# A two-layer decoder step on one core: the sample group's retention step split into dot products with the old states and a later rewriting of the states

## The chip, the core and the metric

The kernel runs on one core of one Trainium2 chip. The metric is the device time of one execution in microseconds. Three runs of the kernel before took 2169.92, 2166.01 and 2169.59 us; the median is 2169.59 us.

## What is computed

Two layers of a decoder trunk, width 2048, in float32. A prompt of 512 tokens and a sample group of 8 sequences with one new token each share all weights and go through the matmuls together, 520 columns. In short:

```python
h = rmsnorm(x); z = h @ W_in                      # b, c, xc, g_conv | q, k, v, g_ret
conv branch: y_c = b * conv3(c * xc) * silu(g_conv)
retention, 4 heads of 256: q, k through rope, k also by 1/16
  prompt: chunked retention from a zero state
  sample: S_new = gamma_h * S + k v^T             # S: 256 x 256 for each layer, head, sequence
          o     = q S_new
o = groupnorm(o) * gn_g * silu(g_ret)
x = x + concat(y_c, y_r) @ W_out
x = x + sigmoid(x @ W_pg) * (p @ W_ple)
```

The outputs are the trunk's result after a final RMSNorm, the last rows of the convolution's input, and the new retention states of both groups. The sample group has 2 x 4 x 8 = 64 states of 256 KB, each read and each written. gamma_h is 1 - 2^(-5-h).

## The kernel before

**Matmuls.** Every float32 product is made of three matmuls: weights and operands are split into a rounded high part and the rest, and high*high, high*low and low*high are added in PSUM (`mm3`, lines 247 to 249). A weight chunk of 128x512 comes in by an SP-queue DMA into the `raw` ring, ScalarE makes its high part (`split_w`, line 229), VectorE its low part (line 230); both go into the `split` ring of 60 tiles of 128x128. Pairs of output tiles are computed by `plain` or by `strassen`, which saves one product of eight and needs sums of weights (VectorE, line 319) and of operands (lines 413 to 416). Operands are split by ScalarE (line 551) and VectorE (line 552).

**Stages of a layer.** The four heads (q, k, v, gate tiles, with the prompt's retention steps in between), eight convolution steps, the out phase (`O` times `wo`, eight pairs of output tiles) and the gate phase (`Gt` times `wg`, eight pairs, seven in the second layer). After the second gate phase a tail computes the last two tiles, the final norm and the outputs. In the profile the heads of layer 0 end near 405 us, its convolutions near 725; its out phase near 914 us and its gate phase near 1076; in layer 1 these are near 1440, 1790, 1975 and 2110 us.

**The sample step.** `sample()` is called at set places of the heads and the convolutions. It runs `sample_step` for one state that an earlier call has loaded, and issues the two loads of the next (`sample_load`): the state, and its q and k broadcast to 128 partitions (`kq`). The step multiplies the state by gamma on ScalarE (line 776, 128x512), adds k times v on VectorE (line 780, two halves of 128x256), stores the new state (line 781, `o_rets`) and takes the dot products with q on VectorE (line 784, two halves, sums into `osum`). In the last convolution step the remaining states are worked off and `sample_norm` (lines 1365 to 1390) does the group norm of `osum`: two pairs of matmuls with a matrix of ones, a power on GpSimd (`rsn`, line 1383), and eight small VectorE products into `gs` (line 1389). `retained` copies `gs` into the columns 512 to 519 of the out phase's operands (line 1064), after it has loaded the prompt's part (`ys`, line 1063).

**What sets the order.** A scheduler places the instructions of each engine by a simulated time line; an engine then works through its list in order and waits, at each instruction, for what it needs. Operations marked `keep` stay in program order on their engine. `middle` and `later` hold functions that are called in the course of the next pair: `later` at two places (`aside`), `middle` at one. All loads and stores of activations and states are issued from GpSimd's queue (`SIDE`), which is in order as well. `Slots` is a pool of 75 buffers of 128x520.

## Time and profile before

| | |
|---|---|
| three runs, median (lowest to highest) | 2169.59 us (2166.01 to 2169.92) |
| profiled execution, its own time by the trace: span from the first to the last instruction | 2167.3 us |
| TensorE matmuls (PE) | 2147.8 us busy, 17861 instructions |
| VectorE (DVE) | 1896.1 us busy, 3849 instructions |
| ScalarE (ACT) | 1264.5 us busy, 2647 instructions |
| GpSimd (POOL) | 430.6 us busy, 746 instructions |
| DMA | 387.31 MB, mean 179 GB/s |
| mean granted TensorE clock | 0.999 |

The profiled execution lies within the three runs, 2.3 us below their median. A busy engine is one with an instruction in flight; SP and the issue of a DMA by SP or ACT aren't counted. A group's mean is the length of one instruction from start to end; consecutive ones overlap a little, so that n of them take a little less than n times the mean. In the view of waits a row names the waiting engine and its tile and line, what it waited for, the sum, the number of waits and the longest. In a table of windows the first number is the length of the stretch, then come the busy time of each engine with its instruction count, the clock, the share of DMA time and GB/s.

### The profile page before, as it was taken

The page shows a single profiled execution, that of the slowest core. Times are in us where ns is not written, and L with a number is a line of the kernel's source. Part 1 is how long each engine was busy: PE and PEld are TensorE (multiplying, and loading weights), DVE is VectorE, ACT ScalarE, POOL GpSimd, SP SyncE. Part 2 cuts the span into 40 slices and gives each one's busy share as a digit, 9 for nine tenths or more (in the row PEclk, how much of TensorE's full clock was granted, in tenths as well). Part 3 has the DMA queues.
Part 4 walks back from the last instruction along what each step waited for, and adds up shares of the span by engine and source line. Part 5 has one row for each costly group of instructions (what it writes and reads, how often), then busy time and mean ns, then how long its engine had stood idle before and what let it go on. Part 6 is the DMA issues. An engine that isn't in the chain of part 4 may idle for free. (4 is left out here: it accounts for less than half of the span.)

```text
span 2167.3 us, 48178 instructions
## 1 busy us (share of the span) xinstructions
PE 2147.8 (99%) x17861; PEld 2142.1 (99%) x17861; DVE 1896.1 (87%) x3849; ACT 1264.5 (58%) x2647; POOL 430.6 (20%) x746
## 2 busy tenths in 40 slices
PE   9999999999999999999999999999999999999998
PEld 9999999999999999999999999999999999999998
DVE  8889988998999987987997988989999998879884
ACT  8656655565555655655765655565645555456565
POOL 2313222211001211200212222231111022011011
PEclk9999999999999999999999999999999999999999
DMA  8555565545543745645645566664464355566455
GB/s 288 171 175 197 181 217 184 178 157 175 158 129 118 238 156 187 215 154 160 215 144 175 172 213 191 189 209 170 151 182 149 120 158 202 176 207 200 128 164 198
DMA packets 182861, 387.31 MB, mean 179 GB/s; under 512 B 25888, under 2 KB 56352, under 8 KB 182624
## 3 DMA queue, kind: packets, MB, share of 16 engines
q1 hardware_dynamic: 128704, 212.98, 31.6%
q0 software_dynamic: 53056, 169.84, 23.8%
q8 instruction: 140, 2.29, 0.4%
q10 hardware_dynamic: 864, 1.39, 0.2%
q14 instruction: 97, 0.79, 0.1%
HBM read 318.96 MB, written 65.15 MB: 177 GB/s over the span
## 5 line engine op out<-in xcount | busy, mean ns | idle before, releaser
L247 PE MATMUL ps_g<-slot,split 128*128 128x260 f32 x5465 | 1531.6, 284 | 7.2 <-ACT slot L307 2.9
L248 PE MATMUL ps_g<-slot,split 128*128 128x260 f32 x5465 | 1534.3, 282 | 0.3 <-DVE slot L555 0.3
L249 PE MATMUL ps_g<-slot,split 128*128 128x260 f32 x5461 | 1519.9, 283 | 0.5 <-DVE split L230 0.5
L229 ACT ACTIVATE split<-raw 128x512 fp32r<-128x512 f32 (+2 forms) x1347 | 777.3, 596 | 583.1 <-DVE raw L319 213.2
L247 PEld LDWEIGHTS ps_g<-slot,split 128*128 128x128 f32 x5465 | 1024.0, 188 | 10.1 <-ACT slot L307 3.7
L248 PEld LDWEIGHTS ps_g<-slot,split 128*128 128x128 f32 x5465 | 1028.5, 188 | 0.5 <-DVE slot L555 0.5
L249 PEld LDWEIGHTS ps_g<-slot,split 128*128 128x128 f32 x5461 | 1019.8, 188 | 1.0 <-DVE split L230 1.0
L230 DVE TENSOR_TENSOR split<-raw,split 128x512 fp32r<-128x512 f32 (+2 forms) x1346 | 849.2, 652 | 172.5 <-PE ps_g L248 85.4
L319 DVE TENSOR_TENSOR raw<-raw 128x512 f32<-128x512 f32 (+1 forms) x660 | 428.9, 660 | 32.5 <-DMA raw<-wi 23.7
L307 ACT ACTIVATE slot<-ps_g 128x260 f32<-128x260 f32 x336 | 127.4, 381 | 140.6 <-PE ps_g L249 122.7
L551 ACT ACTIVATE slot<-slot 128x520 fp32r<-128x520 f32 (+1 forms) x212 | 109.2, 562 | 46.6 <-DVE slot L414 11.1
L552 DVE TENSOR_TENSOR slot<-slot,slot 128x520 fp32r<-128x520 f32 (+1 forms) x212 | 124.4, 620 | 4.1 <-ACT slot L551 3.9
L781 POOL DMA_DIRECT2D o_rets<-slot x64 | 35.3, 552 | 351.6 <-DVE slot L780 131.7
L307 DVE TENSOR_TENSOR slot<-ps_g,slot 128x260 f32<-128x260 f32 x168 | 70.9, 424 | 6.0 <-PE ps_g L249 3.7
L869 POOL DMA_DIRECT2D slot<-hs x64 | 46.2, 724 | 118.7 <-DVE split L230 42.7
L814 POOL DMA_DIRECT2D hs<-slot x64 | 35.6, 556 | 139.3 <-DVE slot L755 61.3
L780 DVE SCALAR_TENSOR_TENSOR slot<-slot,vs,slot 128x256 f32<-128x256 f32 x128 | 56.1, 481 | 4.5 <-ACT slot L776 4.3
L746 DVE TENSOR_TENSOR slot<-slot,slot 128x520 f32<-128x520 f32 x80 | 55.8, 698 | 4.7 <-DMA o_rets<-slot 3.7
L770 POOL DMA_DIRECT2D slot<-sret x64 | 35.5, 554 | 114.6 <-ACT split L229 37.3
L1058 POOL DMA_DIRECT2D slot<-x1s x76 | 40.8, 538 | 87.6 <-PE ps_g L249 27.2
L1209 POOL DMA_DIRECT2D x2s<-slot x30 | 16.4, 545 | 201.6 <-DVE slot L1204 200.6
L771 POOL DMA_DIRECT2D slot<-kq x64 | 34.9, 547 | 106.0 <-DVE slot L876 22.2
(217 smaller groups left out, 1733.8 us busy)
## 6 DMA issues: line engine op xcount, KB each, us to landing
raw<-wi SPq DMA_DIRECT2D x377, 256.0 KB, 3.9
raw<-wo SPq DMA_DIRECT2D x128, 256.0 KB, 5.4
raw<-wg SPq DMA_DIRECT2D x122, 256.0 KB, 4.1
raw<-wi SPq DMA_DIRECT2D x136, 192.0 KB, 4.0
slot<-x1s POOLq DMA_DIRECT2D x76, 260.0 KB, 5.1
slot<-sret POOLq DMA_DIRECT2D x64, 256.0 KB, 4.0
hs<-slot POOLq DMA_DIRECT2D x64, 256.0 KB, 4.0
slot<-hs POOLq DMA_DIRECT2D x64, 256.0 KB, 5.2
```

The source lines that it names most:

```text
L229: S.activation(hi, raw, AF.Copy)
L230: V.tensor_tensor(lo, raw, F(hi), SUB)
L247: PE.matmul(out, wh, xh, start=start, stop=False, skip_group_check=more)
L248: PE.matmul(out, wh, xl, start=False, stop=False, skip_group_check=more)
L249: PE.matmul(out, wl, xh, start=False, stop=stop, skip_group_check=more)
L307: fn(*args)
L319: V.tensor_tensor(out[:, n], x[:, n], y[:, n], op)
L551: keep(S.activation(hi, src[:, n], AF.Copy))
L552: V.tensor_tensor(lo, src[:, n], F(hi), SUB)
L746: V.tensor_tensor(out[:, n], v, table[:, n], MUL)
L780: keep(V.scalar_tensor_tensor(st[:, c], k, vs[:, h, e, b : b + 1], st[:, c], MUL, ADD))
L869: SIDE.dma_start(t[:, :512].rearrange("p (m n) -> p m n", m=2), src)
```

## The change

The dot products are taken with the old state, as q (gamma S) + (q . k) v instead of q (gamma S + k v), and the new state is made later, apart from it.

- In the heads and convolutions `sample_load` loads the old state and, for every second state, the q of two sequences; `sample_step` is only the two dot products on VectorE, with gamma as their constant. The ScalarE product, the k v products and the store are gone from here.
- `retain` multiplies q and k element by element (`qk`), and `vs` is divided by gamma. `sample_norm` begins with two matmuls that sum `qk` over the partitions, two products with `vs` (`own`) and two additions to `osum`.
- In the out and gate phases `update()` does one state's new value in three calls one after the other: `key_load` loads the broadcast k into the right half of a slot; `state_add` makes v k / gamma in both halves by two ScalarE copies with a scale, then issues a GpSimd-queue DMA that adds the old state from DRAM into the slot; `state_out` multiplies the slot by gamma on ScalarE and stores it. Each call works on three states, one in each of these steps. It's called at the middle and at the end of each pair, and in the out phase for m = 2, 6, 10, 14 also from `later`.
- The constants gamma are no longer a part of `vec`.

```diff
@@ constants
+GAMMA = [1.0 - 2.0 ** (-5 - h) for h in range(H)]
...
-    def gam(h):
-        return vec[:, 128 + h : 129 + h]
...
+    qk = const.tile([P, 2, H, NS], F32, name="qk")
...
         def sample_load(h, b):
-            st, kb = get(), get()
+            st = get()
             SIDE.dma_start(st[:, :512], sret[l, h, b])
-            SIDE.dma_start(kb[:, :512], kq[l, h, b].rearrange("c d -> (c d)").partition_broadcast(P))
-            return h, b, st, kb
-
-        def sample_step(h, b, st, kb):
-
-            keep(S.activation(st[:, :512], st[:, :512], AF.Identity, scale=gam(h)))
-            k = kb[:, 256:512]
+            if b % 2 == 0:
+                queries.append(get())
+                src = kq[l, h, b : b + 2, :2].rearrange("b c d -> b (c d)").partition_broadcast(P)
+                SIDE.dma_start(queries[-1][:, :512].rearrange("p (b c) -> p b c", b=2), src)
+            return h, b, st, queries[-1]
+
+        def sample_step(h, b, st, q):
+
             for e in range(2):
                 c = slice(256 * e, 256 * e + 256)
-                keep(V.scalar_tensor_tensor(st[:, c], k, vs[:, h, e, b : b + 1], st[:, c], MUL, ADD))
-            SIDE.dma_start(o_rets[l, h, b], st[:, :512])
-            for e in range(2):
-                c = slice(256 * e, 256 * e + 256)
-                V.tensor_tensor_reduce(k, st[:, c], kb[:, :256], 1.0, 0.0, MUL, ADD, osum[:, e, h, b : b + 1])
-            put(st, kb)
-
-        loaded = []
+                n = slice(256 * (b % 2), 256 * (b % 2) + 256)
+                keep(V.tensor_tensor_reduce(st[:, c], st[:, c], q[:, n], GAMMA[h], 0.0, MUL, ADD, osum[:, e, h, b : b + 1]))
+            put(st)
+            if b % 2:
+                put(q)
+
+        loaded, queries = [], []
...
+        def key_load(h, b):
+            st = get()
+            SIDE.dma_start(st[:, 256:512], kq[l, h, b, 2:].rearrange("c d -> (c d)").partition_broadcast(P))
+            return h, b, st
+
+        def state_add(h, b, st):
+            for e in range(2):
+                c = slice(256 * e, 256 * e + 256)
+                keep(S.activation(st[:, c], st[:, 256:512], AF.Copy, scale=vs[:, h, e, b : b + 1]))
+            SIDE.dma_start(st[:, :512], sret[l, h, b], accum_op=ADD)
+            return h, b, st
+
+        def state_out(h, b, st):
+            keep(S.activation(st[:, :512], st[:, :512], AF.Copy, scale=GAMMA[h]))
+            SIDE.dma_start(o_rets[l, h, b], st[:, :512])
+            put(st)
+
+        keyed, added = [], []
+
+        def update():
+
+            if added:
+                state_out(*added.pop(0))
+            if keyed:
+                added.append(state_add(*keyed.pop(0)))
+            if states:
+                keyed.append(key_load(*states.pop(0)))
+
+        states = [(h, b) for h in range(H) for b in range(NS)]
...
+            V.scalar_tensor_tensor(qk[:, :, h], qks[:, :2, :NS], GAMMA[h], qks[:, 2:, :NS], MUL, MUL)
...
-                V.scalar_tensor_tensor(vs[:, h, e, :], t[:, SEQ:T], 1.0 / 16, rb[:, SEQ:T], MUL, MUL)
+                V.scalar_tensor_tensor(vs[:, h, e, :], t[:, SEQ:T], 1.0 / 16 / GAMMA[h], rb[:, SEQ:T], MUL, MUL)
...
             middle.append(lambda: O.fill(MORE_OUT, 0))
+            middle.append(update)
+            if m % 4:
+                later.append(update)
             zs = pair(O, wo[l], m, m // 2, Gt)
+            update()
...
             middle.append(lambda: Gt.fill(MORE_GATE, 0))
+            middle.append(update)
...
             Gt.fill(MORE_GATE, 0)
+            update()
             Gt.need(m // 2 + 1)
...
+    ps = pr.tile([P, 512], F32, tag="r", name="ps_qk")
+    for d in range(2):
+        PE.matmul(ps[:, :n], ones, qk[:, d].rearrange("p h b -> p (h b)"), start=d == 0, stop=d == 1)
+    own = small.tile([P, 2, H, NS], F32, tag="sq", name="own", bufs=1)
+    for e in range(2):
+        V.tensor_tensor(own[:, e], vs[:, :, e], ps[:, :n].rearrange("p (h b) -> p h b", b=NS), MUL)
+        V.tensor_tensor(osum[:, e], osum[:, e], own[:, e], ADD)
```

Line numbers in the rows below are those of the file that they come from; in the changed file `state_add`'s copies are line 803 and its adding DMA line 804, `state_out`'s product is line 808 and its store 809, and the weight split on ScalarE has become line 230, the operands' split 552.

**First place: GpSimd's queue at the end of layer 0's convolutions.** `yc` rows load or store convolution tiles, `ys` rows load the retention tiles that become operands of the out phase, `rsn` is the power in `sample_norm`. Before:

```order
L781 DMA o_rets<-slot_439_8395 128x512
L1383 TENSOR_TENSOR rsn<-va,half_neg 128x32
L1112 DMA yc<-slot_445_8698 128x520
L1058 DMA slot_466_9255<-yc 128x520
L1058 DMA slot_465_9253<-yc 128x520
L1058 DMA slot_477_9343<-yc 128x520
L1058 DMA slot_478_9345<-yc 128x520
L1118 DMA o_conv<-ncv 128x144
L1063 DMA slot_490_9374<-ys 128x512
L1063 DMA slot_489_9371<-ys 128x512
```

And now:

```order
L1147 DMA o_conv<-ncv 128x144
L1092 DMA slot_474_9227<-ys 128x512
L1092 DMA slot_473_9224<-ys 128x512
L1092 DMA slot_492_9354<-ys 128x512
L1092 DMA slot_491_9351<-ys 128x512
L1104 DMA scv<-sconv 128x128
L1092 DMA slot_498_9370<-ys 128x512
L1092 DMA slot_497_9367<-ys 128x512
L1426 TENSOR_TENSOR rsn<-va,half_neg 128x32
L1092 DMA slot_512_9580<-ys 128x512
L1092 DMA slot_511_9577<-ys 128x512
L797 DMA slot_514_9696<-kq 128x256
```

The power, and with it the end of `sample_norm`, has moved from ahead of `o_conv` to behind the third pair of `ys` loads; two more pairs of these loads and the first key load stand behind it. In layer 1 the power still stands ahead of `o_conv`. Counted in matmuls of TensorE's list, the sum of `sq` in `sample_norm` comes 315 matmuls later than before in layer 0 (5849 in place of 5534) and 249 later in layer 1 (14644 in place of 14395).

**Second place: ScalarE where layer 0's out phase passes into its gate phase.** `split<-raw` is a weight chunk's high part, the slots are operands being split. Before:

```order
L229 ACTIVATE split<-raw 128x512
L551 ACTIVATE slot_649_11578<-slot_646_11570 128x520
L229 ACTIVATE split<-raw 128x512
L551 ACTIVATE slot_660_11828<-slot_597_11344 128x260
L551 ACTIVATE slot_661_11829<-slot_597_11344 128x260
L551 ACTIVATE slot_652_11698<-slot_651_11696 128x520
L551 ACTIVATE slot_655_11704<-slot_654_11702 128x520
L229 ACTIVATE split<-raw 128x512
```

And now:

```order
L230 ACTIVATE split<-raw 128x512 x2
L808 ACTIVATE slot_597_11303<-slot_597_11303 128x512
L803 ACTIVATE slot_652_11552<-slot_652_11552,vs 128x256 x2
L552 ACTIVATE slot_664_11814<-slot_598_11309 128x260
L552 ACTIVATE slot_665_11815<-slot_598_11309 128x260
L552 ACTIVATE slot_666_11820<-slot_599_11310 128x520
L808 ACTIVATE slot_652_11552<-slot_652_11552 128x512
L803 ACTIVATE slot_653_11559<-slot_653_11559,vs 128x256 x2
L552 ACTIVATE slot_656_11684<-slot_655_11682 128x520
L552 ACTIVATE slot_659_11690<-slot_658_11688 128x520
L230 ACTIVATE split<-raw 128x512
L808 ACTIVATE slot_653_11559<-slot_653_11559 128x512
```

Whole updates stand among the same operand and weight splits, several in a row: between `state_add` and `state_out` of one state there are at this place no weight chunk, one, or two.

**Third place: ScalarE within a pair of layer 0's gate phase.** `ps_g` rows copy a product out of PSUM. Before:

```order
L307 ACTIVATE slot_702_12077<-ps_g 128x260
L229 ACTIVATE split<-raw 128x512
L1199 ACTIVATE slot_702_12077<-slot_702_12077 128x520
L229 ACTIVATE split<-raw 128x512 x2
L616 ACTIVATE slot_703_12331<-slot_699_12066 128x520
L307 ACTIVATE ps_g<-ps_g 128x260
L229 ACTIVATE split<-raw 128x512 x3
```

And now:

```order
L803 ACTIVATE slot_709_12272<-slot_709_12272,vs 128x256
L615 ACTIVATE slot_711_12345<-slot_705_12066 128x520
L308 ACTIVATE ps_g<-ps_g 128x260
L230 ACTIVATE split<-raw 128x512 x3
L615 ACTIVATE slot_712_12354<-slot_706_12068 128x520
L808 ACTIVATE slot_709_12272<-slot_709_12272 128x512
L803 ACTIVATE slot_710_12337<-slot_710_12337,vs 128x256
L230 ACTIVATE split<-raw 128x512
L803 ACTIVATE slot_710_12337<-slot_710_12337,vs 128x256
```

Three weight chunks stand here between the last copy of `state_add` and the product of `state_out` on the same slot; between the next two there are eight.

More of the change, by code (lines that the diff above doesn't have):

```diff
@@ L1104, in trunk_kernel @@
                 O.ready = 7
-                sample_norm(nc, small, pr, osum, onesd, half_neg, gs, lambda k: gn_g(l, k))
+                sample_norm(nc, small, pr, osum, qk, vs, ones, onesd, half_neg, gs, lambda k: gn_g(l, k))
             zg, zb = pair(X, wi[l], mt + 2, mt // 2 + 1 - skipped, O)
```

7 lines of the change are left out of this document (4 added, 3 removed).

## The prediction

> **What bounds the kernel now.** I read the page first, then a table of windows with one row for each stage, then TensorE's waits.
>
> ```profile
> span 2167.3 us, 48178 instructions
> PE 2147.8 (99%) x17861; PEld 2142.1 (99%) x17861; DVE 1896.1 (87%) x3849; ACT 1264.5 (58%) x2647; POOL 430.6 (20%) x746
> ```
>
> TensorE is idle for 19.5 us in all. The windows show where; the columns are the stretch, its length, and each engine's busy time with its instructions.
>
> ```profile
> core 0: us, PE busy (x) PEld busy (x) DVE busy (x) ACT busy (x) POOL busy (x), PEclk, DMA share, GB/s
> 85.00:405.00 320.00, 320.00 (x2676) 319.93 (x2676) 287.88 (x637) 188.97 (x416) 89.10 (x155) 1.00 0.60 193
> 405.00:698.00 293.00, 292.06 (x2439) 291.88 (x2438) 267.16 (x534) 161.49 (x327) 40.99 (x61) 1.00 0.49 152
> 698.00:748.00 50.00, 46.68 (x385) 46.07 (x384) 48.04 (x101) 34.11 (x87) 14.95 (x28) 1.00 0.69 226
> 748.00:914.00 166.00, 166.00 (x1386) 165.98 (x1386) 141.40 (x260) 89.97 (x176) 29.00 (x54) 1.00 0.60 194
> 914.00:1076.00 162.00, 162.00 (x1356) 162.00 (x1355) 135.82 (x258) 98.89 (x189) 21.50 (x40) 1.00 0.54 170
> 1076.00:1440.00 364.00, 363.39 (x3033) 362.41 (x3032) 322.92 (x707) 218.82 (x483) 94.87 (x160) 1.00 0.59 183
> 1440.00:1774.00 334.00, 333.12 (x2777) 332.08 (x2776) 307.28 (x622) 187.97 (x389) 51.39 (x79) 1.00 0.50 154
> 1774.00:1808.00 34.00, 32.15 (x267) 31.72 (x266) 33.47 (x74) 23.30 (x66) 10.41 (x20) 1.00 0.79 272
> 1808.00:1975.00 167.00, 167.00 (x1394) 166.99 (x1393) 138.47 (x247) 90.02 (x172) 30.35 (x57) 1.00 0.60 195
> 1975.00:2110.00 135.00, 134.83 (x1122) 134.62 (x1122) 113.05 (x214) 76.16 (x147) 15.59 (x29) 1.00 0.46 145
> 2110.00:2168.00 58.00, 48.34 (x401) 47.60 (x399) 29.53 (x66) 31.46 (x79) 9.81 (x17) 0.97 0.56 193
> ```
>
> A matmul every 320.00/2676 = 119.6 ns in layer 0's heads, where VectorE is busy 90% of the time, and every 166.00/1386 = 119.8 ns in its out phase, where it is 85%: the pace is TensorE's own and doesn't follow VectorE's load. So only idle time can be won. Of that, 9.7 us lie in the tail (58.00 - 48.34) and 2.8 before 85 us (what the other rows leave of 19.5). In the heads and convolutions from 85 to 698 and 1076 to 1774 us it is 0.94 + 0.61 + 0.88 = 2.4 us; at the passages from the convolutions to the out phases (698 to 748, 1774 to 1808) 3.32 + 1.85 = 5.2 us, with VectorE at 96% and 98%; in the out and gate phases proper 0.2 us. The waits name the operand and weight splits:
>
> ```profile
> PE ps_g L247 <- ACT slot L307: 2.9, 4, 1.3
> PE ps_g L247 <- ACT ps_g L307: 1.6, 2, 1.2
> PE ps_g L247 <- ACT split L229: 1.5, 2, 1.3
> ```
>
> The Trainium skill (TensorE: Matmul & The Clock Gate, section Back-to-back issue gap) gives N/2.4 + 2.5 ns for an isolated stream at full clock, 110.8 ns at 260 columns. By that, an estimate, some 17861 x 9 ns = 160 us would be a pace that something holds back; no row here names what, and it isn't VectorE.
>
> **The change part by part.** Rows for what goes and for the nearest to what comes:
>
> ```profile
> L780 DVE SCALAR_TENSOR_TENSOR slot<-slot,vs,slot 128x256 f32<-128x256 f32 x128 | 56.1, 481 | 4.5 <-ACT slot L776 4.3
> L784 DVE CUSTOM_DVE_ANT_0 slot<-slot,slot 128x256 f32<-128x256 f32 x128 | 53.9, 421 | 0.0
> L776 ACT ACTIVATE slot<-slot,vec 128x512 f32<-128x512 f32 x64 | 45.7, 714 | 0.0
> L917 ACT ACTIVATE slot<-ps_kt,vec 128x256 fp32r<-128x256 f32 x32 | 15.0, 468 | 9.2 <-DMA hs<-slot 3.2 <-DVE slot L918 2.5 <-PE ps_kt L913 2.2
> L874 ACT ACTIVATE slot<-slot 128x512 fp32r<-128x512 f32 x48 | 28.7, 624 | 10.1 <-DMA yc<-slot 4.6 <-DVE slot L904 2.4 <-DVE osum L784 2.1
> L1389 DVE SCALAR_TENSOR_TENSOR gs<-dl,vec,gs 128x8 f32<-128x8 f32 x16 | 2.5, 223 | 0.0
> ```
>
> *1. Heads and convolutions.* VectorE loses line 780, 56.1 us, and gets 16 small products and sums of at most 0.223 us, 3.6 us; line 784 stays at 128 times. ScalarE loses 45.7 us, GpSimd's queue 64 stores and half its `kq` loads. TensorE's idle time bounds it: from 0 to -2.4 us. I take **-1.2**, half, since a reordered list has waits of its own.
>
> *2. The passages to the out phases.* They are bound by VectorE, and no sample step lies there. `sample_norm` moves into them. Before, its power ran at these times:
>
> ```profile
> L1383 POOL TENSOR_TENSOR rsn<-va,half_neg x2: 5835/5836/5837, 673.7 to 1743.8; 128x32 f32<-128x32 f32 x2
> 716.85 1.07 POOL L1063 DMA_DIRECT2D slot<-ys  x2 [2.77 <-PE ps_g L249]
> ```
>
> 315 matmuls later at 119.8 ns is 38 us: 711 us in layer 0. There the power stands behind the third pair of `ys` loads, at 716.85 us, and would end near 724; the next two pairs wait up to 5.8 us behind it. VectorE's 18 small instructions of the norm, at most 18 x 0.223 = 4.0 us, fall into the 50 us in which it has 2 us to spare, and ScalarE's copies of `gs` and all operand splits behind them wait for that. In layer 1 it is 249 matmuls, 30 us, so 1774 us: the power is still ahead of the loads, and about ten of the 18 instructions fall into the passage, 2.2 us. Bounds: -5.2 if the relief earlier lets VectorE arrive ahead and all idle time goes, +5.8 (the power's whole delay in layer 0) + 2.2 if it doesn't. I take +2.2 in layer 0 (4.0 less about what VectorE has free) and +0.8 in layer 1: **+3.0**.
>
> *3. Out and gate phases.* ScalarE gets 64 x (2 x 0.468 + 0.624) = 99.8 us. It is busy for 89.97 + 98.89 + 90.02 + 76.16 = 355.0 of 630 us; 455 is 72%, so the work finds room. The wait is another matter. `state_out` waits on ScalarE, in order, for the adding DMA, and the weight splits and operand splits behind it wait too. For the time that an adding DMA takes there is no row; the nearest are
>
> ```profile
> slot<-sret POOLq DMA_DIRECT2D x64, 256.0 KB, 4.0
> slot<-kq POOLq DMA_DIRECT2D x64, 256.0 KB, 4.8
> o_rets<-slot POOLq DMA_DIRECT2D x64, 256.0 KB, 3.1
> slot<-x1s POOLq DMA_DIRECT2D x76, 260.0 KB, 5.1
> slot<-ys POOLq DMA_DIRECT2D x28, 256.0 KB, 5.8
> ```
>
> Between the ends 3.1 (a store) and 8.0 (the plain load twice, as it also reads what it adds to) I take 5, near the loads of the same size. With 0.54 us for the issue (quoted for the tail) it must be covered for 5.5 us. A chunk of weights feeds 12 matmuls, 12 x 119.8 ns = 1.44 us; in the third place three chunks cover 4.3 us. In ScalarE's list 28 of the 64 updates have three chunks or fewer. They are late by about 1.2 us each. That is taken up by two things. Splits run ahead of TensorE, as ScalarE waits for TensorE to free split buffers:
>
> ```profile
> ACT split L229 <- PE ps_g L249: 186.2, 220, 3.9
> ACT split L229 <- DVE raw L319: 213.2, 160, 4.3
> ```
>
> The ring of 60 tiles holds seven split chunks, 10 us. And VectorE has 630 - (141.40 + 135.82 + 138.47 + 113.05) = 101 us free there, 1.6 for each update, 3.2 for each short one. Bounds: -0.2 (no idle time to win) to +29 (the first rival). I take **+1.0**.
>
> The Trainium skill (DMA: Bandwidth & Descriptors, section Anatomy of one DMA) puts one such DMA at 2.0 us + bytes/436e3, 2.6 us for 256 KB; by it no update is late and this term is 0, the sum 2170.7. The trace has 4.0 to 5.1 for such loads, so I don't follow it. The same page's Rules for kernel authors say that an accumulate reads its destination and writes it later; its time no row here shows.
>
> *4. TensorE* gets four matmuls of 32 columns. The four of this kind before are eight in the trace:
>
> ```profile
> L1379 PE MATMUL ps_sv<-sq,onesd 128*128 128x32 f32 x8 | 1.2, 233 | 0.0
> ```
>
> Eight more at the pace of 0.12 to 0.233 us: +1.0 to +1.9; I take **+1.0**.
>
> *5. The tail.* The chain that ended last went through GpSimd's queue:
>
> ```profile
> 2117.33 13.08 issue
> 2130.43 0.54 POOL x2s L1209
> 2132.02 5.61 DMA slot<-x2s
> 2137.65 0.51 ACT slot L1263
> ```
>
> The last store waits for the last sigmoid; now a `state_out` product stands ahead of that sigmoid on ScalarE, and its store ahead in the queue. Its DMA was issued four chunks earlier. From 0 to +5 (a landing in full); I take **+0.6**, one product.
>
> Sum on the profiled execution's own time: 2167.3 - 1.2 + 3.0 + 1.0 + 1.0 + 0.6 = **2171.7 us**. The three runs have their median at 2169.59, 2.3 us above that execution, and scatter by as much, so I leave it there: 0.1% over the median.
>
> **The rivals.**
>
> *Slower: the adding DMA starves the splits.* It decides at a landing of 4.3 - 0.54 + 3.2 = 7.0 us. Above that, each of the 28 short updates costs what is over: at 8.0 us 1.0 us each, 29 us, 2170.7 + 29 = 2200; at 7.5 us 2186. For it: two sources instead of one; at the second place three round trips stand nearly back to back. Against: the slowest plain load of this size quoted above has 5.8 us, and at that place each chunk feeds 24 matmuls (both halves). Chance 0.20.
>
> *Faster: VectorE's relief reaches the passages.* All 2.4 us of part 1 and 4.5 of the 5.2 of part 2 go: 2167.3 - 2.4 - 4.5 + 1.0 + 0.6 = 2162. For it: VectorE at 96% and 98% there. Against: what it loses lies earlier, and the norm comes in. Chance 0.21. A faster pace of TensorE would end on this side too; 119.6 and 119.8 ns at unlike loads of VectorE speak against it: 0.01, from 2162 down.
>
> *Slower: GpSimd's queue blocks operand loads.* The store and the adding DMA wait for ScalarE at the queue's head; `x1s` loads for the gate phase's operands stand behind them. One landing of 5.1 us late at each of the two seams, with part 3 as forecast: 2171.7 + 2 x 3 to 5, about 2179. Against: the loads stand well ahead of their use now. Chance 0.08.
>
> **How the numbers follow.** The forecast has 0.50, and 2166 to 2177 as its own range. About 0.2% is what a measurement of this kernel can tell from no change, that is 2165.3 to 2173.9. Faster: 0.22 + 0.02 of the forecast's half = 0.24. Slower: 0.20 + 0.08 + 0.10 of the forecast = 0.38. The same: 0.38. The range 2161 to 2188 leaves out the upper half of the first rival and a little below.
>
> **What would show it.** Right: TensorE without idle time in 85 to 698 us; more of it than 3.32 us between 698 and 750 us, with the wait of VectorE's `dl` or ScalarE's `gs` copies for `rsn` ahead; ScalarE's waits of line 808 for DMA of 1 to 2 us, some 30 of them, and none of TensorE behind; an adding `slot<-sret` landing in 4 to 6 us. Wrong: that landing above 7 us and TensorE waiting for line 230's splits in the out and gate phases (first rival); idle time at the passages under 2 us (second); ScalarE's line 552 waiting for `x1s` at the seam (third).

## The result, and the profile after

The changed kernel takes 2249.22 us (median of four runs, 2247.86 to 2256.41), the kernel before 2169.66 (four runs beside them): a ratio of 1.0379, 95% interval 1.0362 to 1.0396. It is slower by 3.8%, 82 us by the ratio. The forecast was 2171.7, with a range to 2188. Of one experiment below (e4) two of the four runs, the profiled one among them, were disturbed and are left out.

The page of the profiled run, which took 2256.41 us and is the slowest of the four, begins:

```profile
span 2254.6 us, 48509 instructions
PE 2166.9 (96%) x17869; PEld 2156.9 (96%) x17869; DVE 1862.5 (83%) x3737; ACT 1315.3 (58%) x2775; POOL 517.2 (23%) x842
```

The span grew by 2254.6 - 2167.3 = 87.3 us. TensorE is idle for 2254.6 - 2166.9 = 87.7 us where it was 19.5, so 68.2 of these are idle time; the other 19.1 are longer busy time for the same work and eight small matmuls. The windows by stage, with the columns of those before, show where:

```profile
85.00:405.00 320.00, 320.00 (x2679) 320.00 (x2679) 277.40 (x609) 184.38 (x402) 75.78 (x128) 1.00 0.55 170
405.00:698.00 293.00, 293.00 (x2445) 293.00 (x2444) 261.59 (x502) 158.33 (x315) 25.84 (x40) 1.00 0.44 135
698.00:760.00 62.00, 56.95 (x448) 55.98 (x447) 53.42 (x122) 40.28 (x101) 28.65 (x40) 0.94 0.81 245
760.00:914.00 154.00, 146.67 (x1189) 145.63 (x1189) 115.38 (x209) 89.70 (x186) 53.54 (x91) 0.98 0.79 236
914.00:985.00 71.00, 49.94 (x392) 49.09 (x391) 45.29 (x86) 37.37 (x73) 15.27 (x25) 0.86 0.52 141
985.00:1115.00 130.00, 127.60 (x1060) 127.18 (x1060) 102.84 (x194) 85.70 (x175) 37.64 (x63) 1.00 0.74 225
1115.00:1480.00 365.00, 363.70 (x3034) 362.57 (x3034) 321.93 (x699) 215.85 (x477) 83.15 (x137) 1.00 0.54 168
1480.00:1815.00 335.00, 335.00 (x2805) 335.00 (x2804) 297.48 (x580) 182.46 (x373) 36.21 (x56) 1.00 0.45 136
1815.00:1860.00 45.00, 41.38 (x331) 40.97 (x329) 40.89 (x94) 28.72 (x76) 23.44 (x27) 0.96 0.76 241
1860.00:2010.00 150.00, 142.88 (x1168) 141.52 (x1169) 112.28 (x198) 89.53 (x183) 52.91 (x89) 0.99 0.79 236
2010.00:2070.00 60.00, 37.34 (x285) 36.33 (x285) 39.74 (x76) 30.53 (x57) 17.03 (x30) 0.83 0.60 177
2070.00:2190.00 120.00, 116.15 (x966) 115.62 (x965) 90.09 (x167) 70.63 (x145) 29.19 (x48) 1.00 0.64 191
2190.00:2255.00 65.00, 54.08 (x433) 53.12 (x432) 33.59 (x75) 39.20 (x98) 15.91 (x27) 0.94 0.67 214
```

The heads and convolutions (85 to 698, 1115 to 1815 us) are all but free of idle time. The passages (698 to 760, 1815 to 1860) have 5.05 + 3.62 = 8.7 us. The loss is in the out phases, which had no idle time before: 7.33 + 7.12 us in their courses and 21.06 + 22.66 us at the two seams to the gate phase (914 to 985, 2010 to 2070). There the clock column is at 0.86 and 0.83 too.

The waits of the changed kernel, over the whole program:

```profile
PE ps_g L248 <- ACT slot L1234: 39.5, 2, 20.9
PE ps_g L248 <- DVE slot L308: 11.5, 9, 3.0
PE ps_g L248 <- ACT slot L308: 11.4, 7, 3.5
PE ps_g L248 <- ACT slot L552: 5.7, 5, 2.0
PE ps_g L250 <- DVE split L231: 0.6, 1, 0.6
ACT slot L808 <- DMA slot<-sret: 91.2, 35, 5.4
POOL o_rets L809 <- ACT slot L808: 222.6, 55, 14.9
DVE raw L320 <- DMA raw<-wo: 20.9, 11, 4.5
```

Twice TensorE waits some 20 us for the sigmoid of the first gate pair (line 1234), which frees banks of PSUM, the memory that matmuls write to. Its other larger waits are for instructions that read products out of PSUM (line 308) and for operand splits (line 552); for split weights it waits only 0.6 us (line 231). What keeps the sigmoid is seen in ScalarE's own list at the first seam (start, length, instruction; in brackets the idle time before it and what ended that):

```profile
925.32 0.63 ACT L808 ACTIVATE slot<-slot 128x512 f32<-128x512 f32 x1 [5.36 <-DMA slot<-sret]
...
931.37 0.63 ACT L808 ACTIVATE slot<-slot 128x512 f32<-128x512 f32 x1 [1.53 <-DMA slot<-sret]
...
937.37 0.63 ACT L808 ACTIVATE slot<-slot 128x512 f32<-128x512 f32 x1 [2.85 <-DMA slot<-sret]
...
943.41 0.63 ACT L808 ACTIVATE slot<-slot 128x512 f32<-128x512 f32 x1 [1.96 <-DMA slot<-sret]
...
952.62 1.16 ACT L552 ACTIVATE slot<-slot 128x520 fp32r<-128x520 f32 x2 [3.25 <-DVE slot L415]
953.80 1.28 ACT L1234 ACT_TABLE_LOAD   x1
955.10 1.23 ACT L1234 ACTIVATE slot<-ps_g 128x260 f32<-128x260 f32 x4
```

Four updates follow each other at 6.0 us each: two copies, the issue on GpSimd, the landing, the product. The last operands (line 552) and the sigmoid stand behind them. GpSimd's list at that place shows the gate phase's operand loads (line 1087) between stores that wait for these products:

```profile
938.30 0.56 POOL L809 DMA_DIRECT2D o_rets<-slot  x1 [4.21 <-ACT slot L808]
941.15 0.55 POOL L1087 DMA_DIRECT2D slot<-x1s  x1 [1.05 <-DMA o_rets<-slot]
944.34 0.54 POOL L809 DMA_DIRECT2D o_rets<-slot  x1 [2.64 <-ACT slot L808]
```

The last update's product ends at 944.0 us, eleven before the sigmoid. In between VectorE makes sums of the last operands, with two waits for operand loads, and the splits of 952.62 wait 3.25 us for those sums:

```profile
944.83 0.43 DVE L414 TENSOR_TENSOR slot<-slot 128x260 f32<-128x260 f32 x1 [1.92 <-DMA slot<-x1s]
...
951.77 0.43 DVE L416 TENSOR_TENSOR slot<-slot,slot 128x260 f32<-128x260 f32 x1 [0.22 <-DMA slot<-x1s]
```

### The profile page after: what moved, and what is told of

Same layout as the page of the kernel before. It is cut to its first block, busy times and chain, and to the rows that moved or that the text cites. A ratio compares the mean times of both kernels' runs of the same rounds, so it can differ in the third digit from the quotient of the medians.

```text
span 2254.6 us, 48509 instructions
## 1 busy us (share of the span) xinstructions
PE 2166.9 (96%) x17869; PEld 2156.9 (96%) x17869; DVE 1862.5 (83%) x3737; ACT 1315.3 (58%) x2775; POOL 517.2 (23%) x842
## 3 DMA queue, kind: packets, MB, share of 16 engines
HBM read 335.72 MB, written 65.15 MB: 178 GB/s over the span
## 4 chain that ended last, share of the span: by engine, by line
PE 73%; DMA 11%; issue 6%; DVE 5%; ACT 2%; POOL 2%; SPq 0%; DVEq 0%; POOLq 0%; ACTq 0%
PE ps_g L248 23%; PE ps_g L250 22%; PE ps_g L249 22%; DMA slot<-sret 3%; DMA raw<-wo 2%; DMA raw<-wg 2%; DVE split L231 2%; DMA x2s<-slot 1%; DVE raw L320 1%; ACT split L230 1%; DMA slot<-x1s 1%; ACT slot L803 1%; POOL slot L1087 0%; DMA x1s<-slot 0%; DVE slot L553 0%
## 5 line engine op out<-in xcount | busy, mean ns | idle before, releaser
L248 PE MATMUL ps_g<-slot,split 128*128 128x260 f32 x5465 | 1539.3, 285 | 71.2 <-ACT slot L1234 39.5
L320 DVE TENSOR_TENSOR raw<-raw 128x512 f32<-128x512 f32 (+1 forms) x660 | 425.3, 660 | 56.8 <-DMA raw<-wo 20.9
L769 POOL DMA_DIRECT2D slot<-sret x64 | 35.9, 561 | 297.4 <-ACT split L230 119.5
L808 ACT ACTIVATE slot<-slot 128x512 f32<-128x512 f32 x64 | 40.1, 627 | 91.2 <-DMA slot<-sret 91.2
L898 POOL DMA_DIRECT2D slot<-hs x64 | 46.1, 721 | 156.3 <-PE ps_st L250 69.6
L804 POOL DMA_DIRECT2D slot<-sret x64 | 56.7, 886 | 41.9 <-ACT slot L803 26.7
L803 ACT ACTIVATE slot<-slot,vs 128x256 f32<-128x256 f32 x128 | 63.5, 496 | 2.6 <-DMA slot<-kq 2.3
L308 ACT ACTIVATE ps_g<-ps_g 128x260 f32<-128x260 f32 x121 | 45.0, 372 | 24.3 <-PE ps_g L250 22.2
```

What stands on the lines that cost most here:

```text
L248: PE.matmul(out, wh, xh, start=start, stop=False, skip_group_check=more)
L308: fn(*args)
L320: V.tensor_tensor(out[:, n], x[:, n], y[:, n], op)
L803: keep(S.activation(st[:, c], st[:, 256:512], AF.Copy, scale=vs[:, h, e, b : b + 1]))
L804: SIDE.dma_start(st[:, :512], sret[l, h, b], accum_op=ADD)
```

## The experiments

Four theories. **Theory 1:** the links; ScalarE waits in its list for the round trips of the adding transfers. **Theory 2:** the bytes; the transfers moved into these phases make weights and operands land later, beside ScalarE's added work. **Theory 3:** GpSimd's queue, in which stores and adds that wait stand ahead of operand loads. **Theory 4:** the slots that updates hold and hand on. Each experiment is an edit of the changed kernel. "Over before" is the ratio to the kernel before, timed beside it, less one, times 2169.6 us; the changed kernel itself is 82.2 over. There are 64 updates, 32 in each layer; the expectations below give 128 states, and 192, 128 or 64 instructions by layer, which is twice the real count.

**No updates (e1).**

```diff
-        states = [(h, b) for h in range(H) for b in range(NS)]
+        states = []
```

> Leaves out the 128 new states: no key loads, no ScalarE copies, no adding transfers, no stores in the out and gate phases; the dot products in the heads and the longer norm stay. The changed kernel stands at 2249 us, the one before at 2170. Theory 1 (ScalarE's list, in order, waits for the round trips of the adding transfers, and the sigmoids and splits behind those waits hold TensorE up), theory 2 (the added traffic delays weights and operands) and theory 3 (GpSimd's queue, blocked by stores and adds, delays the operand loads) all put the whole loss into what is left out here: 2158 to 2172, with TensorE idle back at about 20 us. If the heads' part or the norm cost something after all, it stays above 2180.

2171.18 us, ratio 1.0015 (1.0006 to 1.0025): 3.3 us over. So the heads, the dot products, the longer norm and the passages together cost 3.3 us, and the updates 82.2 - 3.3 = 79. TensorE is not idle at all in its convolutions of layer 0, and for 4.2 us in the passage behind them, where the changed kernel has 5.1:

```profile
698.00:760.00 62.00, 57.84 (x455) 57.01 (x454) 55.58 (x128) 37.97 (x95) 23.73 (x33) 0.94 0.71 236
```

**A plain load for the adding one (e2).**

```diff
-            SIDE.dma_start(st[:, :512], sret[l, h, b], accum_op=ADD)
+            SIDE.dma_start(st[:, :512], sret[l, h, b])
```

> The adding transfer becomes a plain load of the same 256 KB onto the same tile, at the same place (leaves out the addition of k v to the state). Theory 1 says that any round trip through a DMA at this place makes ScalarE wait: a plain load is issued in about 0.55 us where the adding one took 0.88, and lands nearly as late, so the loss stays for the most part: 2225 to 2250. If the adding itself (its longer issue, or slower bytes, theory 2 in its narrow form) is what costs, 2170 to 2200.

2220.49 us, 1.0245 (1.0228 to 1.0262): 53.2 over. Both guesses were half right: some 29 us hang on the transfer being an adding one, the larger part doesn't.

**No product, so that ScalarE waits for no transfer (e4, again as e12).**

```diff
-            keep(S.activation(st[:, :512], st[:, :512], AF.Copy, scale=GAMMA[h]))
```

> The product with gamma that ScalarE does on the landed tile is left out, and the store waits for the adding transfer directly, on GpSimd's queue. ScalarE then waits for no adding transfer at all, while GpSimd's queue waits for each of them in its place (some 5 us each). Theory 1: most of the loss goes, 2180 to 2210, the seams from 40 us of TensorE idle to under 10. Theory 3: the loss stays or grows, 2240 to 2290, with the operand loads behind the stores. Theory 2: the bytes are the same, 2240 to 2250.

2229 and 2237 us, 1.0303 (1.0277 to 1.0328): 65.7 over. It was repeated for a trace:

> The variant without the product with gamma once more, for a trace: ScalarE waits for no adding transfer, GpSimd's queue does (leaves out the factor gamma). The first go stood near 2230. Theory 1 alone would have made it 2180 to 2210; near 2230 again means that the wait has only changed its engine: a row of GpSimd waiting for the adding transfers of over 150 us, and operand loads behind it at the seams.

2222.94 us, 1.0253 (1.0236 to 1.0269): 54.9 over. With adding transfers but without ScalarE's wait for them, the time is near that of the plain load with the wait; the same kernel as e4 was 11 us higher. GpSimd now waits in ScalarE's place:

```profile
POOL o_rets L808 <- DMA slot<-sret: 161.8, 59, 8.6
```

**Nothing at the seam (e7).** No update in the last out pair and in the middle of the first gate pair; `later` gets one in each other out pair.

```diff
-            middle.append(update)
-            if m % 4:
-                later.append(update)
+            if m < KT - 2:
+                middle.append(update)
+                later.append(update)
             zs = pair(O, wo[l], m, m // 2, Gt)
-            update()
+            if m < KT - 2:
+                update()
...
-            middle.append(update)
+            if m:
+                middle.append(update)
```

> The same updates, but none in the last pair of the out phase and none in the middle of the first pair of the gate phase; they go to the earlier out pairs, where there was none yet after the second product. All is computed. Theory 1: the two idle times of TensorE at the seams, 18.8 and 21.0 us, shrink to under 8 together and the clock there stays near 1; the out phase before it gets denser in round trips: 2200 to 2222. Theory 2: the same bytes in the same 150 us, so no gain, 2240 to 2255. Theory 3: the operand loads at the seam are no longer behind stores, so it gains here too; the waits on GpSimd's and ScalarE's rows at the seam must tell.

2230.85 us, 1.0298 (1.0277 to 1.0318): 64.7 over. TensorE's waits for the two sigmoids fell from 39.5 us to 8.3, but only 17.5 us of the time went. The denser updates before the seam wait as much (ScalarE's row for the transfers is at 100.8 us), and TensorE stops there instead: between the same matmuls, the courses of the out phases have 12.8 and 10.8 us of idle time in place of 7.3 and 6.2. The seam is where the loss shows, not all of its cause.

**One update later (e3), and both (e8).** The product and the store come a whole update after the adding transfer, with 76 slots and one `qkt` in place of two.

```diff
-            if added:
+            if len(added) > 1 or added and not (keyed or states):
...
+        while added:
+            update()
         if tail:
```

> The product with gamma and the store come one update later, so that a whole further update lies between the adding transfer's issue and the ScalarE instruction that waits for it; same instructions, same bytes, one more slot of 2 KB. All is computed. Theory 1 (round trips in ScalarE's list): that row falls from 91 us to under 30 and the seams to under 15 us of TensorE idle, 2185 to 2212. Theory 2 (bytes): nothing changes, 2240 to 2255. Theory 3 (GpSimd's queue blocked by stores that wait for ScalarE and by long issues): the stores wait less too, but the issues of 0.88 us stay in front of the operand loads, so 2215 to 2240.

> One update later and no update in the last out pair and the middle of the first gate pair, together. All is computed. Theory 1: what is left are the shorter passages before the out phase (some 3 to 6 us) and waits that the denser out phase still has: 2176 to 2198. If it does not come below the variant with one update later alone, the cleared seam adds nothing once the waits are gone. Theory 2: 2240 to 2255.

e3: 2240.28 us, 1.0327 (1.0312 to 1.0342), 70.9 over. e8: 2213.81, 1.0209 (1.0193 to 1.0224), 45.3 over, the best variant that computes everything. In e3 ScalarE's wait for the transfers is down to a third, 30.5 us, and yet only 11 us are won. Counted between the same matmuls of the two traces (the changed kernel's is of its slowest run), its out and gate phases are 22 us shorter than the changed kernel's (662 against 684), and its heads, convolutions and passages 8 us longer; whether the one `qkt` and the 76 slots make them so is not tested. Theory 1 by itself, which said 2185 to 2212 for e3 and 2176 to 2198 for e8, doesn't hold.

**The store from ScalarE's queue (e6).**

```diff
-            SIDE.dma_start(o_rets[l, h, b], st[:, :512])
+            S.dma_start(o_rets[l, h, b], st[:, :512])
```

> The store of a new state is issued from ScalarE's queue, right behind the product that makes it, in place of GpSimd's: 128 waits of GpSimd's queue for ScalarE go, and operand loads and spills no longer stand behind them. All is computed. Theory 3: the seams shrink and it falls to 2195 to 2225. Theory 1: ScalarE still waits for each adding transfer in its list, and now has 64 issues more by layer; the adding transfers and key loads are issued a little earlier: 2235 to 2260.

2265.82 us, 1.0456 (1.0436 to 1.0475): 98.9 over, above what either theory said. GpSimd is rid of its waits for the product, but its adding transfers now wait for ScalarE (129.0 and 76.3 us by two rows of its waits). It doesn't test theory 3 cleanly, since the queue stays tied to ScalarE.

**VectorE's additions, no round trip (e5), and with a cleared seam (e15).** The old state and the key are loaded one update ahead, VectorE adds as in the kernel before, ScalarE multiplies, GpSimd stores.

```diff
+            SIDE.dma_start(st[:, :512], sret[l, h, b])
+            SIDE.dma_start(kb[:, :256], kq[l, h, b, 2:].rearrange("c d -> (c d)").partition_broadcast(P))
...
-                keep(S.activation(st[:, c], st[:, 256:512], AF.Copy, scale=vs[:, h, e, b : b + 1]))
-            SIDE.dma_start(st[:, :512], sret[l, h, b], accum_op=ADD)
+                keep(V.scalar_tensor_tensor(st[:, c], kb[:, :256], vs[:, h, e, b : b + 1], st[:, c], MUL, ADD))
```

> No adding transfer: in the out and gate phases the old state and the key are loaded plainly one update ahead, VectorE does the two additions of k v (two instructions of 128x256 for each state), ScalarE the product before or after, and GpSimd stores. All is computed, with the same bytes to within the key loads. No round trip is left, since what an update touches was loaded an update earlier. Theory 1: 2172 to 2192, the rest being the passages and VectorE's 128 additions by layer in phases where it was idle for 101 us. Theory 2 (bytes): 2235 or more. If VectorE becomes the bound, 2192 to 2215 with its share over 0.95 in the out phase.

> VectorE's additions in place of the adding transfers, as in the variant that stood at 2220 us, and no update in the last out pair and the middle of the first gate pair, as in the variant that cleared the seam. All is computed. The seam held 10.8 and 7.3 us of TensorE idle there; if clearing it takes those away, and the clock near it comes back, 2195 to 2208; if the denser out phase gives it back, 2212 to 2222. It doesn't come below the kernel before in either case, since without any update it is 2171.

e5: 2220.40 us, 1.0243 (1.0227 to 1.0258), 52.7 over. e15: 2229.42, 1.0277 (1.0261 to 1.0292), 60.1 over. No adding transfer and none waited for on arrival, and still some 50 us. Here a cleared seam makes it worse, and both ranges for e15 are missed. So far theory 1, in the form of a wait for an adding transfer, explains at most the step from about 53 to 82.

**One suspect at a time (e9, e10, e11).** From e1 upwards: two slots held and nothing done with them; the old state loaded and stored with no arithmetic; the keys, the copies and the product with neither the adding transfer nor the store.

```diff
@@ e9, with states = []
+        held = [get(), get()]
         for m in range(0, KT, 2):
...
+        put(*held)
         if tail:
@@ e10
+        def state_load(h, b):
+            st = get()
+            SIDE.dma_start(st[:, :512], sret[l, h, b])
+            return h, b, st
...
         def state_out(h, b, st):
-            keep(S.activation(st[:, :512], st[:, :512], AF.Copy, scale=GAMMA[h]))
             SIDE.dma_start(o_rets[l, h, b], st[:, :512])
@@ e11
-            SIDE.dma_start(st[:, :512], sret[l, h, b], accum_op=ADD)
...
-            SIDE.dma_start(o_rets[l, h, b], st[:, :512])
```

> Leaves out the new states as the first experiment does, and holds two slots unused from the start of the out phase to the end of the gate phase, as the updates do (5 free slots in place of 7 in the full out pairs, none in place of 2 in the gate pairs). The first experiment stood at 2171 us; with VectorE's additions and no round trip for ScalarE it was still 2220. Theory 4 (the slots that updates hold make every other tile wait for a store or a load to land): a good part of those 49 us appears without any update, 2190 to 2220. If slots do not matter: 2168 to 2177.

> The update's transfers without its arithmetic: each old state is loaded plainly and stored again one update later, through the same two or three slots; no key, no ScalarE or VectorE instruction (leaves out the additions and the factor gamma). No engine but GpSimd's queue touches it. Theory 1 (ScalarE waiting in its list): 2171 to 2182. Theories 2 to 4 together (bytes, GpSimd's queue, slots in flight): 2190 to 2215, with waits of DVE and ScalarE for weights or for slots still being stored.

> The changed kernel without the adding transfer and without the store: keys are loaded, ScalarE makes its two copies and the product, and the slot goes back (leaves out the old state and the output of the new one). ScalarE's 192 instructions by layer stay, with no round trip to wait for but the key's. If ScalarE's own added time in its list were the cost: 2195 to 2225. Theory 1 in its form as a wait for the transfer: 2171 to 2185. Theory 4 by slots held alone would show here too, as two slots stay taken: 2190 or more.

e9: 2170.93 us, 1.0014 (1.0005 to 1.0024), 3.0 over: the number of free slots costs nothing. e10: 2187.77, 1.0090 (1.0075 to 1.0106), 19.5 over, so 16 above e1. e11: 2185.51, 1.0079 (1.0062 to 1.0096), 17.1 over, so 14 above e1. Both lie between the ranges that were expected. Together they would make 33 over; with the wait and a plain load it is 53, with the adding one 82.

**Both loads without a link (e13).** ScalarE works on the key's tile; GpSimd loads and stores the old state on another (with 76 slots and one `qkt`, as in e3).

```diff
-            st = get()
-            SIDE.dma_start(st[:, 256:512], kq[l, h, b, 2:].rearrange("c d -> (c d)").partition_broadcast(P))
+            kb = get()
+            SIDE.dma_start(kb[:, 256:512], kq[l, h, b, 2:].rearrange("c d -> (c d)").partition_broadcast(P))
...
+            st = get()
-                keep(S.activation(st[:, c], st[:, 256:512], AF.Copy, scale=vs[:, h, e, b : b + 1]))
-            SIDE.dma_start(st[:, :512], sret[l, h, b], accum_op=ADD)
+                keep(S.activation(kb[:, c], kb[:, 256:512], AF.Copy, scale=vs[:, h, e, b : b + 1]))
+            SIDE.dma_start(st[:, :512], sret[l, h, b])
...
-            keep(S.activation(st[:, :512], st[:, :512], AF.Copy, scale=GAMMA[h]))
+            keep(S.activation(kb[:, :512], kb[:, :512], AF.Copy, scale=GAMMA[h]))
```

> All of the update's instructions, but on two tiles that have nothing to do with each other: ScalarE makes its two copies and the product on the key's tile, and GpSimd loads the old state plainly onto a second tile and stores it one update later (leaves out the addition and the factor gamma; the new state that is stored is the old one). Same count of instructions and bytes as the variant with a plain load in place of the adding one, which stood at 2220 us, and one slot more. If the links are the loss: the two single loads add up, 2195 to 2207. If the two loads together are enough: 2215 to 2225.

2225.19 us, 1.0260 (1.0240 to 1.0279): 56.4 over. The links through the data are not what the 20 us over the sum are: without them it isn't faster than e2.

**Adding transfers, no product, the store later (e14).** e3 without the line of the product.

> The adding transfers stay, the product with gamma is left out, and the store comes one update later, so that neither ScalarE nor, for most updates, GpSimd's queue waits for an adding transfer to land (leaves out the factor gamma). With the store one update earlier it stood at 2223 us. If waits for the landing are the loss: 2190 to 2207. If it is the adding transfer itself (its issue of 0.88 us on GpSimd, its bytes): 2215 to 2225.

2249.99 us, 1.0373 (1.0355 to 1.0390): 80.9 over, 26 more than e12, above both ranges. But the run doesn't test what it was made for. The store isn't held in program order, and the scheduler put it back: in GpSimd's list 51 of the 64 stores stand behind their own adding transfer with no later one between, where e12 has 54 and e3, whose product is held, 7. The list begins so:

```profile
732.61 0.92 POOL L804 DMA_DIRECT2D slot<-sret  x1
738.40 0.55 POOL L808 DMA_DIRECT2D o_rets<-slot  x1 [4.29 <-DMA slot<-sret]
738.94 0.92 POOL L804 DMA_DIRECT2D slot<-sret  x1
```

So GpSimd waits for landings as long as in e12 (164.3 us against 161.8). That two kernels with nearly the same order of adds and stores lie 26 us apart is a caution for every step below. Between the same matmuls, 8 us of it lie in the heads and convolutions, 7 in the passages and 10 in the out and gate phases; why is not settled.

**Tiles of the updates' own (e17),** again with one `qkt`.

```diff
-SPLIT = 60
+SPLIT = 52
...
+    own = [const.tile([P, 512], F32, name=f"own{i}") for i in range(3)]
...
-            st = get()
+            st = own.pop(0)
...
-            put(st)
+            own.append(st)
```

> The changed kernel, all computed, with three tiles kept for the updates, so that the slots of operands, inputs and spills are handed round exactly as without updates; the ring of split weights is shorter for it, 52 blocks in place of 60. If slots handed on while a store or load is in flight are a main part of the loss: 2195 to 2220. If the queues are, GpSimd's and ScalarE's: 2240 to 2260, as before or a little worse for the shorter ring.

2237.72 us, 1.0321 (1.0295 to 1.0347): 69.6 over. It lies between the two ranges: the handing round of slots is worth the 12.6 us won, and more if the shorter ring costs something, but it is no main part.

**Past SBUF (e16, e18).** e11 with two transfers from DRAM to DRAM by update, which need no tile and wait for no engine; in e18 they are held at their places with `keep`.

```diff
-            SIDE.dma_start(st[:, :512], sret[l, h, b], accum_op=ADD)
+            SIDE.dma_start(spare[l, h, b], sret[l, h, b])
...
-            SIDE.dma_start(o_rets[l, h, b], st[:, :512])
+            SIDE.dma_start(o_rets[l, h, b], sret[l, h, b])
```

> ScalarE's copies and product on the key's tile stay, and each update's two transfers of 256 KB go from DRAM to DRAM, the old state to a spare place and to the output, past SBUF (leaves out the addition and the factor gamma). Same issues on GpSimd's queue, at the same places, with bytes of the same order, but no transfer waits for a tile or an engine and no tile waits for a transfer but the key's. ScalarE's work with the keys alone stood at 2185. If the bytes beside that work were the loss: 2215 to 2230. If waits in GpSimd's queue and tiles in flight are: 2185 to 2200.

e16: 2232.08 us, 1.0296 (1.0271 to 1.0321), 64.2 over, but the transfers aren't at the places meant: free of waits, the scheduler put them at the start of the program. There they cost no less. From 85 to 325 us, in layer 0's heads, e1 does 2010 matmuls (first row) and e16 1680, 330 x 0.1196 = 39 us of work less:

```profile
85.00:325.00 240.00, 240.00 (x2010) 240.00 (x2009) 208.42 (x457) 138.65 (x299) 57.95 (x97) 1.00 0.56 177
85.00:325.00 240.00, 217.52 (x1680) 212.46 (x1679) 181.85 (x398) 119.72 (x265) 89.48 (x166) 0.94 0.71 236
```

> As the variant past SBUF, with the transfers held in program order, at the places of the changed kernel's adds and stores in GpSimd's list (leaves out the addition and the factor gamma). ScalarE's work with the keys alone stood at 2185, with the transfers through tiles of their own at 2225. If the bytes beside ScalarE's work were the loss: 2212 to 2228. If waits in GpSimd's queue and tiles still being loaded or stored are: 2183 to 2200.

e18: 2223.48 us, 1.0262 (1.0245 to 1.0279), 56.8 over. With no tile, no landing and no engine to wait for, the transfers cost 39.7 us on top of e11; through tiles of their own in e13 it was 56.4 - 17.1 = 39.3. They aren't quite the same bytes: by the pages e18 reads 352.50 MB from DRAM and writes 81.93, where the changed kernel, e2 and e13 have 335.72 and 65.15. The same out phase, 1461 or 1462 matmuls long, in e1, e11, e18 and the changed kernel:

```profile
775.20:950.20 175.00, 175.00 (x1462) 175.00 (x1461) 145.49 (x268) 96.92 (x187) 27.56 (x53) 1.00 0.56 183
```

```profile
776.10:956.40 180.30, 176.90 (x1462) 176.69 (x1462) 149.61 (x275) 121.51 (x248) 38.45 (x72) 0.99 0.60 193
```

```profile
776.60:969.00 192.40, 179.17 (x1461) 177.80 (x1460) 149.54 (x276) 122.35 (x249) 57.02 (x108) 0.97 0.68 230
```

```profile
776.20:987.30 211.10, 182.71 (x1462) 180.82 (x1462) 148.32 (x272) 119.60 (x245) 66.59 (x111) 0.94 0.72 211
```

TensorE's idle time goes 0, 3.4, 13.2, 28.4 us. One thing that the third row has is a late landing of the weights, which come by another queue (SP's) than these transfers. In the kernel before, in e1 and in e18:

```profile
raw<-wo SPq DMA_DIRECT2D x128, 256.0 KB, 5.4
```

```profile
raw<-wo SPq DMA_DIRECT2D x128, 256.0 KB, 4.7
```

```profile
raw<-wo SPq DMA_DIRECT2D x128, 256.0 KB, 7.1
```

ScalarE and VectorE wait 86.9 us for weights of the two phases in e18, half of it VectorE's sums (line 320):

```profile
DVE raw L320 <- DMA raw<-wo: 23.3, 14, 3.2
DVE raw L320 <- DMA raw<-wg: 22.6, 9, 4.1
```

The kernel before has 16.0 us of such waits, e1 3.7 and the changed kernel 48.3. But TensorE doesn't run out of split weights. It waits for other things, in e18 so:

```profile
PE ps_g L248 <- ACT slot L1235: 18.9, 3, 9.4
PE ps_g L248 <- DVE slot L308: 14.6, 11, 2.9
PE ps_g L250 <- DVE split L231: 0.3, 1, 0.3
```

The second row is how late weights get to TensorE. Some 3 us or less before the end of each of these eleven waits VectorE has waited for weights at a sum (line 320), and the instruction that reads PSUM (line 308) stands behind that sum in VectorE's list. For example:

```profile
2147.39 0.56 DVE L320 TENSOR_TENSOR raw<-raw 128x384 f32<-128x384 f32 x1 [1.34 <-DMA raw<-wg]
2147.86 0.42 DVE L308 TENSOR_TENSOR slot<-ps_g,slot 128x260 f32<-128x260 f32 x1
```

e11 has no such wait, the changed kernel 11.5 us. The first row is the sigmoid at the seams (6.4 us in e11): ScalarE does five updates there in 10 us, with products at 912.89, 914.86, 917.47, 920.01 and 921.60 us, between operand splits that stand ahead of the sigmoid.

Other runs with the same total have other shares. e2 waits 32.7 us for the two sigmoids and 3.2 for VectorE's line 308, e13 13.1 and 1.2, with 20.0 and 31.9 us of waits for weights; e10 has weights landing late too (6.2 us) but only 6.3 us of waits for them, and still costs 16. So the weights' landing is one path of several.

## Why the prediction was wrong

The steps of the runs, over before: 3.3 without updates (e1); 17.1 with ScalarE's instructions and the keys (e11); 56.8 with the transfers' bytes and issues at their places (e18), and as much with plain transfers through tiles (e2 53.2, e5 52.7, e13 56.4), with links or without, though TensorE waits for different things in these; 82.2 with adding transfers that ScalarE waits for. Take away either the adding (e2) or the wait (e12 54.9, as e4 65.7), and most of the last step goes. The 26 us between e12 and e14 say how far a single such difference can be trusted.

1. *Heads and convolutions, forecast -1.2:* right. From 85 to 698 and 1115 to 1815 us TensorE is idle for 1.30 us; the stretches before had 2.4.
2. *Passages, +3.0:* right in size. 8.7 us of idle time against 5.2; without updates (e1) it is 4.16 + 3.02 = 7.2.
3. *Out and gate phases, +1.0, bounds -0.2 to +29:* **this step failed;** it measured 79 us. It failed in three places.
   - It read ScalarE's room from an average ("455 is 72%, so the work finds room"), and 14 us of loss come from those instructions and the key loads with no adding transfer at all (e11).
   - It priced the adding transfer by its own landing, and put what the moved loads and stores do to everything else in these phases at nothing, without a reason. That is the largest part: 16 us alone (e10) and 40 us beside ScalarE's work, with no wait of ScalarE for them (e18, e13).
   - It let a late split be taken up by the ring of split weights and VectorE's free time. The ring did hold: TensorE waits 0.6 us for split weights. What ScalarE's and VectorE's waits held up were the instructions that read PSUM, the operand splits and the sigmoid, for which TensorE waits directly (39.5 + 11.5 + 11.4 + 5.7 us). And it took all 28 short updates as 1.2 us late, as with three chunks, though by ScalarE's list in the trace 13 of them have two or fewer; at the seam they come in a row.
4. *Four matmuls, +1.0:* can't be told from these runs. With them TensorE is busy 1.1 us longer than before in e9 and 3.9 in e1.
5. *The tail, +0.6:* up to the end of each span, 64.6 - 54.08 = 10.5 us idle against 57.3 - 48.34 = 9.0. (The prediction's 9.7 counts 0.7 us behind the end.)

Terms 1, 2, 4 and 5 make +3.4; e1 measured 3.3 (1.3 to 5.4). That it agrees so closely is partly luck: the passages of e1 have less idle time than forecast, but in the first of them 455 matmuls take 57.84/455 = 127 ns each, at a clock of 0.94, where 119.6 was the pace, and these 3.4 us are in no term.

Two of the signs for "right" came close to true and misled: ScalarE's line 808 waits 35 times, 2.6 us each on average (forecast: some 30 times, 1 to 2 us), and the adding transfers land in 5.6 us by the median (4 to 6).

*The first rival* (the adding transfer starves the splits) had the side right, and price and path wrong. It was to decide at a landing of 7.0 us (its 3.2 us of VectorE's time for each short update is 101/28 = 3.6 by its own figures, which would make it 7.4); 11 of the 64 landings are above 7.0, the longest 9.9, and TensorE did not wait for line 230's splits. Its top price of 29 is near the last step, 27 to 29 us, but that step isn't shown to be its mechanism. *The third rival* (GpSimd's queue at the seams) is in the trace: operand loads stand behind waiting stores, and VectorE waits for them on the way to the sigmoid, 1.92 + 0.22 us in the last stretch of the first seam. How much of the seams' 21 to 23 us is its own stays open, since in e6 the queue stayed tied to ScalarE. *The second* (faster) fell: in e1 the idle time of the heads and convolutions goes down by about 1.2 us, and that of the passages up by 2.0.

Left open: how the 40 us divide into bytes and GpSimd's 64 issues a layer (e18 has both), and by which waits they get to TensorE in the changed kernel itself; why e14 is 26 us slower than e12; and why the heads and passages of e3 are 8 us longer.

No variant beats the kernel before: the best that computes everything (e8) is 45 us over, and even without any update the rest is 3.3 over, so nothing was there to win.

## What to carry to other kernels

Before you move work into a phase that has "room", look at the phase's slack by place and not by average: how far the loads run ahead, what stands behind the new instructions in each in-order list, and where several of them fall together. A buffer covers only what passes through it: here the ring of split weights held, and the sigmoids and the reads of PSUM that share the lists with the splits did not. Price a moved transfer by what it does to the transfers that are already there, and to the engines that wait for them. Two loads that cost 16 and 14 us alone cost 53 together, with no link between them (e13); that they spend the same lead is a guess. And look in the trace at where the scheduler has put an instruction before you read an experiment on its place.

## What the runs showed of the hardware

An adding transfer of 256 KB from DRAM into SBUF takes GpSimd 0.886 us to issue where a plain one takes 0.540 (means of 64, changed kernel and e2, line 804), and lands later. Line 804's landings in the changed kernel and in e2:

```profile
DMA to landing us min/median/max: 3.9/5.6/9.9
```

```profile
DMA to landing us min/median/max: 2.8/4.6/9.0
```

By the fit of the Trainium skill (DMA: Bandwidth & Descriptors, section Anatomy of one DMA) it would be 2.6 us for 256 KB, an estimate; the runs, with other transfers beside, show about twice that.

TensorE slows after a stall. After the first seam's 18.6 us of idle time (936.9 to 955.5 us), ten microseconds hold 60 matmuls, 158 ns each, and the next ten 85:

```profile
955.00:965.00 10.00, 9.46 (x60) 9.46 (x61) 6.26 (x13) 6.67 (x16) 2.71 (x5) 0.73 0.55 175
965.00:975.00 10.00, 10.00 (x85) 10.00 (x84) 4.62 (x7) 4.50 (x9) 1.44 (x2) 1.00 0.79 223
```

That is 60 x (158 - 119.6) ns = 2.3 us on top of the stall. The Trainium skill (TensorE: Matmul & The Clock Gate, section What's actually happening) has the clock halved after an idle window of about 3.4 us and restored after as long a busy one; the trace's clock is at 0.50 from 939.9 to 960.4 us, so it falls 3.0 us after the stall begins and is back 4.9 us after it ends, which agrees roughly.
